# A decoder layer on one core, with 29 series of unread products behind its last output

## The chip, the cores and the metric

The kernel runs on one core of one Trainium2 chip. TensorE (PE) multiplies: its stationary operand is loaded by a weight load (PEld), its moving operand streams through, and the result goes to a bank of PSUM. VectorE (DVE), ScalarE (ACT) and GpSimd (POOL) work on elements; SyncE (SP) mostly issues DMAs. The metric is the device time of one execution in microseconds.

## The reference

The reference is one layer of a hybrid decoder on a sequence of 256 rows and a width of 2048: a combined projection, two groups of eight heads, an output projection, and a feed-forward part with a causal convolution of width 3.

```python
h = rmsnorm(x, pre_mix_gain)
q_sb, k_sb, v_sb, q_dl, k_dl, v_dl = split(h @ w_in)
o_sb = stick_breaking_attention(q_sb, k_sb, v_sb)
o_dl = dilated_attention(rope(q_dl), rope(k_dl), v_dl)
x = x + rmsnorm(concat(head_rmsnorm(o_sb), head_rmsnorm(o_dl)) @ w_out, post_mix_gain)
u = rmsnorm(x, pre_ffn_gain) @ w_up
gate, val = split(causal_conv3(u) + conv_b)
x = x + rmsnorm((gelu(gate) * val) @ w_down, post_ffn_gain)
```

## The kernel before

All matrices are float32. Each is split in two float32r parts, a high part wh (ACT copies the loaded tile, L89) and a low part wl (DVE subtracts, L96), and so are the activations; a product of the layer is then three products of TensorE: high by high, high by low, low by high. The weights stream in from memory in tiles of 128 x 1024 (SP's queue) and are consumed once, in this order: values, queries and keys with the attention between them, output projection, the up projection (chunks "up", mm_stationary at L98 to L112), and the down projection (class Down).

In mm_stationary the weights are the stationary operand: 128 columns of a high part against 512 moving columns (L111), and of a low part against 256 (L109). Low parts of the kinds "qk" and "up" start LOW_AT = 80 floats into their buffer; nothing else about L109's operands is shifted. In Down the weights move, 512 columns at a time, and the feed-forward activations are stationary: yp holds the two float32r parts of 13 pairs of blocks (yp0 the high ones, yp1 the low ones, 13 x 7 x 128 columns each), yt those of the single blocks. L629, L630 and L631 are the three products there. The bank of a product is of the pools ps_mm or ps_at, four banks each.

The end is written out by hand. The last units of the down projection are held back (HELD), and their products are made bank by bank, so that rows can be closed (L649), squared and scaled while the next bank is multiplied. The last bank is made in two halves of 256 columns, p9. The calls put() write the results and issue the stores (L693 and L695). Elsewhere a scheduler sets each engine's order from the program's text; instructions that go through pin() keep the order that they are written in.

Of the kernel before, what the change touches and what calls it, by code (L numbers as in the profile page):

```python
# [9 lines left out]
F32 = mybir.dt.float32  # L10
F32R = mybir.dt.float32r
BF16 = mybir.dt.bfloat16
# [4 lines left out]
P = 128  # L17
# [34 lines left out]
def layer_kernel(ctx: ExitStack, tc: tile.TileContext, a, out: bass.AP):  # L52
    nc = tc.nc
    V, A, T, G = nc.vector, nc.scalar, nc.tensor, nc.gpsimd
# [5 lines left out]
    ps_at = ctx.enter_context(tc.tile_pool(name="ps_at", bufs=4, space=PSUM))  # L60
# [206 lines left out]
    first = [None, None]  # L267
# [220 lines left out]
    phB = None  # L488
# [40 lines left out]
    class Down:  # L529
# [123 lines left out]
        def run(self):  # L653
# [89 lines left out]
            put(1, 1536, 2048, r, V, nc.scalar)  # L743
            pinned[0] = False

    down = Down()
    for i, (kind, p, s, _, w) in enumerate(chunks):
        parts = ahead(i, 0 if (kind, p, s) == ("out", 3, 3) else SPLITS)
        if kind == "v":
            if s == 0:  # L750
                pool, tag = (ps_at, "at") if p == 1 else (ps_mm, "mm")
# [26 lines left out]
        elif kind == "qk":  # L778
            ps = ps_mm.tile([P, 2, S], F32, tag="mm", name="mmqk")
# [9 lines left out]
        elif kind == "out":  # L789
# [14 lines left out]
            else:  # L804
                pinned[0] = True
                up0 = []
                r = [None, None]
# [94 lines left out]
                phB = ctx.enter_context(tc.tile_pool(name="phB", bufs=2))  # L902
                yt = [phB.tile([P, len(SINGLES), S], F32R, name=f"yt{i}", bufs=1) for i in range(2)]
                yp = [phB.tile([P, NPAIR, 7, P], F32R, name=f"yp{i}", bufs=1) for i in range(2)]
        else:
            ps = ps_mm.tile([P, 2, S], F32, tag="mm", name="mmu")
# [24 lines left out]
    rows = Rows(fg, "d", 5)  # L931
    tc.keep_in_program_order(A.preload_act_table_set("natural_log_exp_and_others"))
    down.run()


def _constants():
# [69 lines left out]
```

## Time and profile before

| what | us |
|---|---|
| median of 2 runs | 1094.28 |
| the runs | 1093.95 to 1094.6 |
| span of the profiled execution | 1092.2 |
| PE busy | 1079.7 |
| PE idle up to 400 us, and from there to 1083.33 | 3.7 and 0.1 |
| from PE's last start in the layer to the end of the span | 9.0 |

The profiled execution has a time of its own only as its span, from the first to the last instruction; the median of the runs lies 2.1 us above it. A row of the timeline has start, duration, engine, line, operation, the tiles written and read, and in brackets the idle time before it. A matmul's duration is its latency; several are in flight at once. A row that ends in x2 or more merges instructions that follow each other.

### The profile page before, as it was taken

The numbers are of one execution on the slowest core, as the hardware profiler recorded it, in microseconds if no ns is written. First come the engines' busy times: TensorE is split into PE (matmuls) and PEld (weight loads), VectorE is DVE, ScalarE is ACT, GpSimd is POOL, SyncE is SP. The second block draws the span as 40 slices with busy tenths as digits, with TensorE's granted clock in tenths as the row PEclk, the third lists the DMA queues.
The fourth block names the chain that finished last, engine by engine and source line by source line (L and its number), as shares of the span: only waits on it lengthen the run. The fifth ranks groups of instructions, "written<-read, shape, count | busy, mean of one in ns | idle before, by whom it ended". The sixth has DMA issues, their size and how long they took to land.

```text
span 1092.2 us, 16194 instructions
## 1 busy us (share of the span) xinstructions
PE 1079.7 (99%) x5855; PEld 932.8 (85%) x5855; DVE 878.4 (80%) x1371; ACT 668.4 (61%) x1046; POOL 5.3 (0%) x12
## 2 busy tenths in 40 slices
PE   9999999999999999999999999999999999999996
PEld 6898888988888888888888888888888888888885
DVE  6577776876876588988888888888888899889887
ACT  6656656656754476665666665666666566666665
POOL 0000000000000000000000000000000000000001
PEclk9999999999999999999999999999999999999998
DMA  8979768888889756656565656566556677767775
GB/s 309 391 255 310 275 231 305 266 283 288 265 274 307 260 191 212 193 194 193 193 193 193 193 193 193 193 193 194 193 193 193 216 235 249 253 219 249 250 242 209
DMA packets 75393, 257.79 MB, mean 236 GB/s; under 512 B 8496, under 2 KB 9520, under 8 KB 74544
## 3 DMA queue, kind: packets, MB, share of 16 engines
q1 hardware_dynamic: 74880, 256.22, 70.6%
q8 instruction: 46, 0.75, 0.3%
q10 hardware_dynamic: 432, 0.53, 0.1%
q14 instruction: 35, 0.29, 0.1%
HBM read 238.89 MB, written 17.83 MB: 235 GB/s over the span
## 4 chain that ended last, share of the span: by engine, by line
PE 97%; ACT 1%; issue 0%; DMA 0%; DVE 0%; SPq 0%; DVEq 0%; ACTq 0%
PE mmu L111 28%; PE mmu L109 14%; PE mmqk L111 11%; PE p L629 7%; PE p L630 7%; PE p L631 7%; PE mmqk L109 5%; PE mmo L151 3%; PE mmo L154 3%; PE mmo L150 3%; PE mmv L151 3%; PE mmv L154 3%; PE mmv L150 3%; PE mmu L117 1%; DMA raw<-in_w_v 0%
## 5 line engine op out<-in xcount | busy, mean ns | idle before, releaser
L96 DVE TENSOR_TENSOR wl<-raw,wh 128x1024 fp32r<-128x1024 f32 (+1 forms) x408 | 480.3, 1188 | 125.0 <-ACT wh L89 96.9
L89 ACT CAST wh<-raw 128x1024 fp32r<-128x1024 f32 (+1 forms) x408 | 414.2, 1024 | 171.5 <-PE mmu L111 42.3
L111 PE MATMUL mmu<-hT,wh 128*128 128x512 f32 x1344 | 318.2, 390 | 0.0
L111 PEld LDWEIGHTS mmu<-hT,wh 128*128 128x128 f32 x1344 | 249.2, 188 | 50.0
L109 PE MATMUL mmu<-hT,wl 128*128 128x256 f32 x1344 | 166.7, 276 | 0.0
L109 PEld LDWEIGHTS mmu<-hT,wl 128*128 128x128 f32 x1344 | 162.0, 188 | 3.5
L111 PE MATMUL mmqk<-hT,wh 128*128 128x512 f32 x512 | 121.8, 390 | 0.0
L111 PEld LDWEIGHTS mmqk<-hT,wh 128*128 128x128 f32 x512 | 94.9, 188 | 19.0
L502 ACT ACTIVATE cv<-u,par 128x256 f32<-128x256 f32 x86 | 51.9, 603 | 90.2 <-DVE u L500 90.0
L631 PE MATMUL p<-wl,yp 128*128 128x512 f32 x182 | 70.9, 390 | 0.0
L630 PE MATMUL p<-wh,yp 128*128 128x512 f32 x182 | 70.8, 389 | 0.0
L629 PE MATMUL p<-wh,yp 128*128 128x512 f32 x182 | 70.8, 389 | 0.0
L109 PE MATMUL mmqk<-hT,wl 128*128 128x256 f32 x512 | 68.3, 281 | 0.0
L109 PEld LDWEIGHTS mmqk<-hT,wl 128*128 128x128 f32 x512 | 63.8, 188 | 1.7
L503 DVE SCALAR_TENSOR_TENSOR cv<-u,par,cv 128x255 f32<-128x255 f32 x86 | 41.4, 481 | 29.0 <-ACT cv L502 29.0
L630 PE MATMUL p<-wh,yt 128*128 128x512 f32 (+1 forms) x140 | 53.6, 383 | 0.0
L629 PE MATMUL p<-wh,yt 128*128 128x512 f32 (+1 forms) x140 | 53.6, 383 | 0.0
L631 PE MATMUL p<-wl,yt 128*128 128x512 f32 (+1 forms) x140 | 53.5, 383 | 0.0
L135 ACT COPY half<-mmu 128x256 f32<-128x256 f32 x86 | 31.8, 370 | 35.2 <-PE mmu L109 21.7
L89 ACT CAST wh<-room 128x1024 fp32r<-128x1024 f32 x26 | 27.4, 1054 | 39.2 <-PE p L630 37.4
L150 PE MATMUL mmv<-wh,hT 128*128 128x512 f32 x128 | 49.8, 391 | 0.7 <-ACT hT L234 0.7
L151 PE MATMUL mmv<-wh,hT 128*128 128x512 f32 x128 | 50.0, 391 | 0.4 <-DVE hT L281 0.2
(178 smaller groups left out, 1248.2 us busy)
## 6 DMA issues: line engine op xcount, KB each, us to landing
raw<-in_w_up SPq DMA_DIRECT2D x172, 512.0 KB, 3.8
raw<-in_w_qk SPq DMA_DIRECT2D x64, 512.0 KB, 5.8
raw<-in_w_dn SPq DMA_DIRECT2D x60, 512.0 KB, 4.5
raw<-in_w_o SPq DMA_DIRECT2D x32, 512.0 KB, 4.8
raw<-in_w_v SPq DMA_DIRECT2D x28, 512.0 KB, 5.6
t<-in_w_dn SPq DMA_DIRECT2D x26, 512.0 KB, 5.0
t_kept<-t SPq DMA_DIRECT2D x26, 512.0 KB, 4.1
raw<-t_kept SPq DMA_DIRECT2D x26, 512.0 KB, 4.3
```

What stands on the lines that cost most here:

```text
L89: pin(A.copy(wh, raw))
L96: pin(V.tensor_tensor(wl, raw, wh.bitcast(F32), op=ALU.subtract))
L109: T.matmul(ps[:, 0, :], w, h[:, k, 0, :], **edge)
L111: T.matmul(ps, w, h[:, k, :, :], **edge)
L150: T.matmul(ps[t], hi[:, k, tc_], ws, start=(first and i == 0 and j == 0), stop=False)
L151: T.matmul(ps[t], lo[:, k, tc_], ws, start=False, stop=False)
L154: T.matmul(ps[t], hi[:, k, tc_], wl[:, j * 512:(j + 1) * 512], start=False, stop=(last and i == len(parts) - 1 and j == n - 1))
L502: A.activation(cv, u, AF.Identity, scale=cw(2), bias=par[:, P_CB + f:P_CB + f + 1])
L503: V.scalar_tensor_tensor(cv[:, 1:], u[:, :S - 1], cw(1), cv[:, 1:], op0=ALU.mult, op1=ALU.add)
L629: T.matmul(ps, yh, wh[:, cs], start=key not in self.begun, stop=False)
L630: T.matmul(ps, yl, wh[:, cs], start=False, stop=False)
L631: T.matmul(ps, yh, wl[:, cs], start=False, stop=self.left[key] == 0)
```

## The change

Behind down.run() the kernel calls a new function, more_products(). It takes one bank of ps_at (probe), clears a tile of bf16 zeros, and calls row() 29 times. A call makes 12 products (the first makes 24) that all write that bank; four moving places 2048 floats apart in yp0 take turns, and eight stationary places 1024 floats apart in yp1. The argument `at` moves the stationary operand by up to 112 floats. The moving operand is 512, 256 or 128 columns in one run; some series begin it 4, 8 or 16 floats further, some take it in two or four blocks with gaps, some read one block of 128 columns four times or one of 32 sixteen times, and one takes the zeros for both operands. All but the last two series set the start flag at their first product alone, and those two at each. The bank is read by nothing, and nothing of the layer is changed.

```diff
+    def more_products():
+
+        f0, f1 = (y.rearrange("p m r c -> p (m r c)") for y in yp)
+        ps = ps_at.tile([P, 512], F32, tag="at", name="probe")
+        zeros = phB.tile([P, 512], BF16, tag="cv0", name="zeros", bufs=1)
+        V.memset(zeros, 0.0)
+
+        def row(moving, at, n=12, first=False, w=None):
+            for i in range(n):
+                m = moving(2048 * (i % 4))
+                st = f1[:, at + 1024 * (i % 8):at + 1024 * (i % 8) + P] if w is None else w
...
+                T.matmul(dst, st, m, start=first or i == 0, stop=True, skip_group_check=True)
+
+        flat = lambda n, off=0: lambda b: f0[:, b + off:b + off + n]
+        blocks = lambda a, n, gap: lambda b: f0[:, b:b + a * gap].rearrange("p (a g) -> p a g", a=a)[:, :, 0:n]
+        same = lambda a, n: lambda b: f0[:, b:b + n].rearrange("p (o n) -> p o n", o=1).broadcast_to([P, a, n])
+        row(flat(512), 0, 24)
+        for at in (0, 16, 32, 48, 64, 80, 96, 112):
+            row(flat(512), at)
+        row(flat(512, 4), 0)
+        row(flat(512, 8), 0)
+        row(flat(512, 16), 16)
+        row(blocks(2, 256, 384), 0)
+        row(blocks(4, 128, 256), 0)
+        row(same(4, 128), 0)
+        row(same(16, 32), 0)
+        row(lambda b: zeros, 0, w=zeros[:, 0:P])
+        for at in (0, 16, 32, 48, 64, 80, 96, 112):
+            row(flat(256), at)
+        row(flat(128), 0)
+        row(flat(128), 80)
+        row(flat(512), 0, first=True)
+        row(flat(256), 80, first=True)
...
     down.run()
+    more_products()
```

In the built program, TensorE's queue before ends with the last products of the second half of bank p9 and the branch out of the program:

```order
L629 MATMUL p_10764<-wh,yt_4098 128x256
L630 MATMUL p_10764<-wh,yt_4099 128x256
L631 MATMUL p_10764<-wl,yt_4098 128x256
L629 MATMUL p_10764<-wh,yt_4098 128x256
L630 MATMUL p_10764<-wh,yt_4099 128x256
L631 MATMUL p_10764<-wl,yt_4098 128x256
L1002 UNCONDITIONAL_BRANCH
```

Behind the same last L631 there stand now the new products, of which the rows below are the first and the last (the zeros' products between them come one by one, each with a weight load of its own):

```order
L631 MATMUL p_10764<-wl,yt_4098 128x256
L763 MATMUL probe<-yp_4100,yp_4101 128x512 x204
L763 LDWEIGHTS zeros
L763 MATMUL probe<-zeros 128x512
...
L763 MATMUL probe<-yp_4100,yp_4101 128x256 x96
L763 MATMUL probe<-yp_4100,yp_4101 128x128 x24
L763 MATMUL probe<-yp_4100,yp_4101 128x512 x12
L763 MATMUL probe<-yp_4100,yp_4101 128x256 x12
L1043 UNCONDITIONAL_BRANCH
```

Nothing of the layer has moved at that end. The first of the new products waits for DVE, which has to read the first half of p9 (L649) out of the bank that probe gets; no later one waits for another engine but the first on the zeros, which needs their MEMSET.

That MEMSET the scheduler has put far ahead, on DVE, where the up projection gives way to the pairs of the down projection (room is the tile of sums, wl the low parts):

```order
 L612 TENSOR_TENSOR room_9001<-raw_9064,raw_8950 128x512
-L614 TENSOR_TENSOR room_9001<-room_9001,raw_9014 128x512
+L751 MEMSET zeros_10905 128x256
 L96 TENSOR_TENSOR wl_9072<-raw_8950,wh_9070 128x1024
 L96 TENSOR_TENSOR wl_9080<-raw_9014,wh_9078 128x512
+L614 TENSOR_TENSOR room_9001<-room_9001,raw_9014 128x512
 L96 TENSOR_TENSOR wl_9091<-raw_9064,wh_9089 128x1024
 L96 TENSOR_TENSOR wl_9101<-room_9001,wh_9099 128x1024
```

The MEMSET stands where L614 stood, and L614 has gone behind two L96. On TensorE, one L629 of bank p7 and one L631 of bank p5 have changed places a little later; DMAs and the other engines keep their order.

More of the change, by code (lines that the diff above doesn't have):

```diff
@@ L744, in run @@
             pinned[0] = False
+    def more_products():
[7 more added lines that the diff above has]
+                st = f1[:, at + 1024 * (i % 8):at + 1024 * (i % 8) + P] if w is None else w
+                cols = 1
+                for d in m.shape[1:]:
+                    cols *= d
+                dst = ps[:, 0:cols]
+                if len(m.shape) == 3:
+                    dst = dst.rearrange("p (a b) -> p a b", a=m.shape[1])
+                T.matmul(dst, st, m, start=first or i == 0, stop=True, skip_group_check=True)
[19 more added lines that the diff above has]
+        row(flat(256), 80, first=True)
     down = Down()
```

## The prediction

> **What bounds the kernel now.** I read four views in this order: the page's span and busy shares, to see which engine sets the length; the timeline of the last microseconds, since the change stands there; the timeline at four places where TensorE runs products of known widths, for the slot that one product takes; and the waits around 876 us, where the built program moves one DVE instruction. First the page:
>
> ```profile
> span 1092.2 us, 16194 instructions
> PE 1079.7 (99%) x5855; PEld 932.8 (85%) x5855; DVE 878.4 (80%) x1371; ACT 668.4 (61%) x1046; POOL 5.3 (0%) x12
> PEclk9999999999999999999999999999999999999998
> L111 PE MATMUL mmu<-hT,wh 128*128 128x512 f32 x1344 | 318.2, 390 | 0.0
> ```
>
> PE is busy 99% of the span at the full granted clock. The 390 ns of an L111 product is its latency, not its cost in a stream: the next one starts long before it ends. So a product is priced by the distance between starts. The end of the timeline, with the DVE read that frees the new products' bank:
>
> ```profile
> 1080.46 0.28 PE L629 MATMUL p<-wh,yt 128*128 128x256 f32 x1
> ...
> 1082.46 0.42 DVE L649 TENSOR_TENSOR room<-p,room 128x256 f32<-128x256 f32 x1
> ...
> 1083.21 0.28 PE L631 MATMUL p<-wl,yt 128*128 128x256 f32 x1
> ...
> 1085.76 2.06 DVE L693 SCALAR_TENSOR_TENSOR room<-room,rs,x1q 128x512 f32<-128x512 f32 x3
> ...
> 1087.20 1.00 ACTq L695 DMA_DIRECT2D out<-room  x2
> out<-room ACTq DMA_DIRECT2D x2, 256.0 KB, 2.5
> ```
>
> PE starts its last product at 1083.21. Behind it, 8.9 us pass without PE: DVE finishes the rows, the stores are issued until 1088.20 and land about 2.5 us later (last row, from the DMA view), near 1090.7; the span ends 1.5 us behind that. The new products stand on PE alone, and nothing of the layer waits for them.
>
> **What the change costs, part by part.** The program after it holds 360 more products: 216 of f32r 512 columns wide (the first series has 24, sixteen more have 12 each: 24 + 16 x 12), 108 of 256 columns (nine series), 24 of 128 (two), and 12 of bf16 512 columns on zeros (one); 29 calls of row in all. They are one queue on one engine, so the sum of their slots is the length of the block.
>
> Slots. These rows give them; starts are in the first column:
>
> ```profile
> 1060.04 0.39 PE L629 MATMUL p<-wh,yp 128*128 128x512 f32 x1
> ...
> 1074.32 0.39 PE L629 MATMUL p<-wh,yt 128*128 128x512 f32 x1
> 859.81 3.45 PE L109 MATMUL mmu<-hT,wl 128*128 128x256 f32 x29
> 67.25 0.59 PE L378 MATMUL z<-qk 128*128 128x256 f32 x2
> 67.68 0.38 PE L379 MATMUL z<-qk 128*128 128x128 f32 x2
> 67.90 0.22 PE L380 MATMUL z<-mskb,idb 128*128 128x128 bf16 x1
> 67.96 0.22 PE L381 MATMUL z<-mskb,idb 128*128 128x128 bf16 x1
> L109 PE MATMUL mmu<-hT,wl 128*128 128x256 f32 x1344 | 166.7, 276 | 0.0
> L378 PE MATMUL z<-qk 128*128 128x256 f32 x16 | 4.8, 380 | 0.0
> L379 PE MATMUL z<-qk 128*128 128x128 f32 x16 | 3.1, 274 | 0.0
> ```
>
> - 512 columns, f32r. From 1060.04 to 1074.32 stand 21 rounds of L629, L630, L631, 63 products: 14.28 / 63 = 0.2267 us. 216 x 0.2267 = 48.97 us.
> - 256 columns. Two prices. The 24 products from 1080.46 to 1083.21 make 23 slots: 2.75 / 23 = 0.1196 us. The 29 of L109 make 28 slots in 3.45 less the last one's 0.28: 0.1132 us. The difference between them that the code shows is the stationary operand's place: L109 loads low parts that LOW_AT puts 80 floats further. So the row at place 0 gets 0.1196 (12 products, 1.44 us), the two rows at place 80 get 0.1132 (24, 2.72 us), and the six other places the middle, 0.1164 (72, 8.38 us): 12.54 us. Bounds by the two prices: 12.2 and 12.9.
> - The same 6 ns could be saved by the 84 wide products at the seven places other than 0; no row has a wide product with its stationary there alone, so the bounds are 0 and 84 x 0.0064 = 0.54 us less, or as much more should a place be worse than 0. I take half of the saving, 0.27 less: 48.7 us for the wide ones.
> - 128 columns, f32r: the trace has none. Two bounds: the two L379 records start 0.38 - 0.27 = 0.11 us apart, the bf16 pair L380 and L381 0.06. I take 0.11, since f32 weights stand there as here: 24 x 0.11 = 2.64 us (1.44 by the lower; 2.87 if they cost as much as 256 columns, 0.1196).
> - bf16 zeros, 512 columns: between the f32r slot of 0.2267 and the 0.1196 of half the width. The two records of L378 start 0.59 - 0.38 = 0.21 apart; I take 0.22: 2.64 us (1.44 to 2.72).
> - Unseen patterns: moving operands begun 4, 8 and 16 floats further, in blocks with gaps (two rows), and one block read over and over (two rows). Every moving operand here is one plain run, so no row prices these. Below, they cost what a plain run does; above, I let an operand that is read badly take two slots: 12 x 0.2267 = 2.7 us a row, 19.0 us for all seven. I take nothing, because the slot of plain runs follows their width (0.2267 against 0.1196 for half), and these patterns have the same width.
>
> The block: 48.7 + 12.54 + 2.64 + 2.64 = 66.5 us.
>
> The Trainium skill, TensorE: Matmul & The Clock Gate, section Back-to-back issue gap, gives a warm slot of the columns over 2.4 per ns plus 2.5 ns: 216, 109 and 56 ns. By it, an estimate, the block would be 228 x 0.216 + 108 x 0.109 + 24 x 0.056 = 62.4 us, 4.1 less. Here the trace has 227 and 113 to 120 ns in f32r, so I go by the trace.
>
> Where the block starts. In the order, the first new product waits for one thing, the DVE read of bank p9 that begins at 1082.46 and takes 0.42 us; it is over at 1082.88, before the last product of the layer starts. So it starts one slot behind that one, at 1083.21 + 0.12 = 1083.33. All issue slots are over at 1083.33 + 66.5 = 1149.83. The last product's latency reaches 0.28 - 0.11 = 0.17 us further: 1150.0.
>
> What lies beside it. The stores, 8.9 us, now run under the block and cost nothing; their cover is 58 us deep. In exchange the program's end follows PE. What stands behind the last thing waited for is bounded by 0 and the 1.5 us that the span has behind the landing; these waits of SP lie in it:
>
> ```profile
> SPq L1002 <- DMA out<-room: 2.6, 1, 2.6
> SPq L1002 <- PEq L1002: 0.6, 2, 0.4
> ```
>
> The second row is SP meeting PE at the close, 0.6 us in two waits; I take 0.9 for the whole close. Span: 1150.9.
>
> The zeros. The MEMSET stands on DVE in the stretch where products of the pairs begin, and the scheduler has put L614 behind two L96 there, as the order shows. These rows are from before:
>
> ```profile
> L240 DVE MEMSET warm<- x1: 272/272/272, 0.9 to 0.9; 128x256 uint32 x1
> 875.55 0.69 DVE L614 TENSOR_TENSOR room<-room,raw 128x512 f32<-128x512 f32 x1
> 876.16 2.96 DVE L96 TENSOR_TENSOR wl<-raw,wh 128x1024 fp32r<-128x1024 f32 x3
> 877.26 1.05 ACT L89 CAST wh<-room 128x1024 fp32r<-128x1024 f32 x1
> 877.43 0.19 PEld L631 LDWEIGHTS p<-wl,yp 128*128 128x128 f32 x1 [0.29 <-DVE wl L96]
> ```
>
> PEld waits 0.29 us for an L96 there. In place of a 0.69 us L614, a 0.27 us MEMSET now stands ahead of it, so it can come 0.42 us sooner and the wait can go. L614 comes about 1.5 us later (0.27 and two L96), and the CAST of room that waits for it with it; its products are two units further on, which covers that. Bounds: -0.3 (the wait goes) and +0.3 (the CAST is late next). I take 0. The swap of an L629 and an L631 of two banks on PE moves no work; also 0.
>
> Sum: the span grows by 1150.9 - 1092.2 = 58.7 us. The profiled execution is 1092.2 and the median of the runs 1094.28, 2.1 above; I keep that distance. Forecast: 1094.3 + 58.7 = **1153.0 us**, 5.4% slower.
>
> **The rivals.**
>
> 1. Patterns or places read badly. If one to three of the rows with unseen patterns take double slots, 2.7 to 8.2 us are added: 1155.7 to 1161.2. If all seven do, 1172. For it: no row shows such a pattern, and 6 ns hang on a place already. Against it: the price needed is forty times that.
> 2. The small prices all fall at their lower ends: 84 x 0.0064 off the wide rows at new places (half of it is in already), 256 columns at 0.1132, 128 at 0.06, zeros at 0.12: -0.27 - 0.3 - 1.2 - 1.2, about 1150.0. By the gap rule above, 1148.9; there the place of an operand would have to explain the whole 10 ns between 216 and 227 in every row, but rows at place 0 are what the 227 was measured on.
> 3. The other side, not slower: the products do not run. The block would have to shrink to 1092.2 + 21.9 - 0.9 - 0.17 - 1083.33 = 29.7 us to stay within 2%, 0.083 us a product on average; the narrowest kind alone takes 0.11. Only dropping them gets there, since their bank is never read: 1094.3. Against it: the built program holds all 360 behind the last L631. Nor can earlier waits swallow them: up to 1083.33 PE idles only about 3.6 us.
> 4. The clock falls to half for the block: another 66 us, 1219. The PEclk row shows a fall only in the last slice, where PE has nothing; here PE does not stop.
>
> **How the numbers follow.** The forecast with its small bounds (1150.0 to 1155): 0.77. Rival 1: 0.15 for one to three rows, 0.03 for more. Rival 2 below 1150.0, the gap rule in it: 0.03. Rival 3: 0.01. Rival 4: 0.01. The range takes in the small ends and rival 1 up to three rows: 1149 to 1161, which leaves out about 0.1. A measurement of this kernel tells 2%, some 22 us, from no change. Slower: 0.985; within: 0.01; faster: 0.005, for something unforeseen.
>
> **What would show it.** After: PE's products rise by 360 records, 6215 in all; L631's last start stays near 1083.2 and the first new one follows within 0.2 us; the wide rows go at 0.220 to 0.230 us, 256 columns at 0.113 to 0.120, 128 at 0.11; PE's last end lies near 1150, the last store lands where it did, and the span ends some 0.9 us behind PE. The wait of L631 at 877.43 shrinks or stays. Wrong would be: a row whose slots are far off 0.227 (rival 1; the row says which operand), slots of 0.06 at 128 columns, a granted clock under 1.00 in the block, a start held back by a wait.

## The result and the profile after

The changed kernel takes 1153.85 us, the median of two runs from 1153.58 to 1154.12, against 1094.28: a ratio of 1.0548, with a 95% interval of 1.0531 to 1.0565. The forecast was 1153.0.

The page of the changed kernel, its first lines:

```profile
span 1152.3 us, 16914 instructions
PE 1148.0 (100%) x6215; PEld 990.0 (86%) x6215; DVE 878.7 (76%) x1372; ACT 668.0 (58%) x1046; POOL 6.7 (1%) x12
DVE  6577766868866789888888888888889888988600
ACT  6656646646644576655656656656556666666400
L763 PE MATMUL probe<-yp,yp 128*128 128x512 f32 (+2 forms) x348 | 65.6, 350 | 0.0
```

PE has 360 products more, and DVE one instruction. The two digit rows show where the time went: DVE and ACT are done in the last two slices, some 58 us, in which only PE works. The next rows are of PE's timeline, around the start of the block and at its end:

```profile
1083.38 0.28 PE L630 MATMUL p<-wh,yt 128*128 128x256 f32 x1
1083.50 0.28 PE L631 MATMUL p<-wl,yt 128*128 128x256 f32 x1
1083.62 0.86 PE L763 MATMUL probe<-yp,yp 128*128 128x512 f32 x3
...
1150.27 1.22 PE L763 MATMUL probe<-yp,yp 128*128 128x256 f32 x9
```

The block begins one narrow slot behind the last product of the layer, at 1083.62; the row has no idle time in brackets, so no wait stands ahead of it. The nine products of the last row begin at 1150.27 and are over 1.22 us later, at 1151.49. Who waits for that, the waits of SP's queue tell (what waited and for what; us in total, times, the longest):

```profile
SPq L1043 <- PE probe L763: 60.2, 1, 60.2
SPq L695 <- DVE room L649: 10.0, 1, 10.0
SPq L1043 <- DMA out<-room: 2.6, 1, 2.6
...
SPq L1043 <- PEq L1043: 0.6, 2, 0.4
```

The wait for the stores is 2.6 us as before. Behind it SP now waits 60.2 us for the last new product, and then the same 0.6 us of closing waits follow. The stores have moved nowhere; they are simply no longer last.

Each window below holds one series of the block, from its first start to that of the next (so 12 slots; the x counts products in flight at the edges too). The columns are the window, its length, PE's busy time with the number of products, the granted clock, and the DMAs:

```profile
1089.08:1091.80 2.72, 2.72 (x13) 1.00 0.52 191
1091.80:1094.59 2.79, 2.79 (x13) 1.00 0.01 3
1097.39:1100.14 2.75, 2.75 (x13) 1.00 0.00 0
1111.21:1114.00 2.79, 2.79 (x13) 1.00 0.00 0
1119.52:1122.25 2.73, 2.73 (x13) 1.00 0.00 0
1127.69:1130.53 2.84, 2.84 (x13) 1.00 0.00 0
1130.53:1132.95 2.42, 2.42 (x13) 1.00 0.00 0
```

They are, in this order, the wide products at place 0, at 16 and at 48, the moving operand 4 floats further, two blocks with a gap, 32 columns read sixteen times, and the zeros. Over twelve slots, 2.72 us is 0.2267, 2.79 is 0.2325 and 2.84 is 0.2367. No pattern takes a second slot, and the clock is 1.00 throughout. All series follow, with the mean distance of starts within each, in ns. In four of them, the zeros, 256 columns at place 0, 128 columns at place 0 and the last one of 512 columns, the first distance belongs to the change from one kind of product to the next (227, 308, 59 and 289 ns) and is left out of the mean:

```
512 columns, place 0 (24, then 12)      227.9   226.6
512 columns, places 16 32 48 64         233.5   233.0   228.9   227.7
512 columns, places 80 96 112           233.5   233.0   228.9
moving +4, +8; both +16                 232.5   233.4   226.9
2 blocks of 256, 4 of 128 with gaps     227.7   226.6
128 four times, 32 sixteen times        226.6   236.5
zeros, bf16                             216
256 columns, places 0 16 32 48          119     117.8   119.1   117.7
256 columns, places 64 80 96 112        119.3   117.8   119.1   117.7
128 columns, places 0 and 80            111.7   111.6
start at each: 512 at 0, 256 at 80      227     117.8
```

The wide slots repeat after 64 floats: 16 and 80 agree, 32 and 96, 48 and 112. Where both operands are shifted by 16 floats, the slot here is that of place 0.

### The profile page after: what moved, and what is told of

Read it like the earlier page. It is cut to its first block, busy times and chain, and to the rows that moved or that the text cites. A ratio compares the mean times of both kernels' runs of the same rounds, so it can differ in the third digit from the quotient of the medians.

```text
span 1152.3 us, 16914 instructions
## 1 busy us (share of the span) xinstructions
PE 1148.0 (100%) x6215; PEld 990.0 (86%) x6215; DVE 878.7 (76%) x1372; ACT 668.0 (58%) x1046; POOL 6.7 (1%) x12
## 4 chain that ended last, share of the span: by engine, by line
PE 97%; DMA 1%; ACT 1%; issue 0%; DVE 0%; SPq 0%; ACTq 0%
PE mmu L111 26%; PE mmu L109 13%; PE mmqk L111 10%; PE p L631 6%; PE p L630 6%; PE p L629 6%; PE probe L763 6%; PE mmqk L109 5%; PE mmo L151 3%; PE mmo L154 3%; PE mmo L150 3%; PE mmv L154 2%; PE mmv L150 2%; PE mmv L151 2%; DMA mg<-in_xT 1%; PE mmu L117 1%
## 5 line engine op out<-in xcount | busy, mean ns | idle before, releaser
L96 DVE TENSOR_TENSOR wl<-raw,wh 128x1024 fp32r<-128x1024 f32 (+1 forms) x408 | 480.2, 1187 | 125.3 <-ACT wh L89 96.9
L89 ACT CAST wh<-raw 128x1024 fp32r<-128x1024 f32 (+1 forms) x408 | 414.0, 1024 | 170.1 <-PE mmu L111 42.7
L109 PE MATMUL mmu<-hT,wl 128*128 128x256 f32 x1344 | 166.7, 277 | 0.0
L109 PEld LDWEIGHTS mmu<-hT,wl 128*128 128x128 f32 x1344 | 162.1, 188 | 3.5
L631 PE MATMUL p<-wl,yp 128*128 128x512 f32 x182 | 70.9, 390 | 0.0
L629 PE MATMUL p<-wh,yp 128*128 128x512 f32 x182 | 70.8, 389 | 0.0
L109 PE MATMUL mmqk<-hT,wl 128*128 128x256 f32 x512 | 68.3, 281 | 0.0
L763 PE MATMUL probe<-yp,yp 128*128 128x512 f32 (+2 forms) x348 | 65.6, 350 | 0.0
L109 PEld LDWEIGHTS mmqk<-hT,wl 128*128 128x128 f32 x512 | 63.8, 188 | 1.7
L763 PEld LDWEIGHTS probe<-yp,yp 128*128 128x128 f32 x348 | 56.1, 188 | 9.1
L629 PE MATMUL p<-wh,yt 128*128 128x512 f32 (+1 forms) x140 | 53.6, 383 | 0.0
L631 PE MATMUL p<-wl,yt 128*128 128x512 f32 (+1 forms) x140 | 53.5, 383 | 0.0
```

The lines of the kernel that those rows point to most:

```text
L89: pin(A.copy(wh, raw))
L96: pin(V.tensor_tensor(wl, raw, wh.bitcast(F32), op=ALU.subtract))
L109: T.matmul(ps[:, 0, :], w, h[:, k, 0, :], **edge)
L629: T.matmul(ps, yh, wh[:, cs], start=key not in self.begun, stop=False)
L631: T.matmul(ps, yh, wl[:, cs], start=False, stop=self.left[key] == 0)
L763: T.matmul(dst, st, m, start=first or i == 0, stop=True, skip_group_check=True)
```

## Experiments

All kernels below keep the layer as it is and differ only behind it. They replace the body of more_products by calls of one helper, in which ss and ms are the steps of the stationary and of the moving places, in floats:

```diff
+        def series(n, cols, at, ss=1024, ns=8, ms=2048, nm=4, off=0, stop=True):
+            for i in range(n):
+                m = f0[:, off + ms * (i % nm):off + ms * (i % nm) + cols]
+                st = f1[:, at + ss * (i % ns):at + ss * (i % ns) + P]
+                T.matmul(ps[:, 0:cols], st, m, start=i == 0, stop=stop or i == n - 1, skip_group_check=True)
```

The theory at the start was that of the prediction: the time is the sum of the slots, less what the stores cover. Its first rival was that nothing is covered, or that the products slow the closing rows. Open were the layer's end, which came 0.29 us later than in the trace of before, and the place: at 80 the narrow products took 0.1178 us and not the 0.1132 of L109.

**The kernel before, once more.** No edit.

> The kernel before, once more, for the spread of its own trace. If the layer's end moves from execution to execution, its last product starts anywhere between 1083.1 and 1083.6 us here; if the 0.29 us by which the layer ended later in the changed kernel is the change's doing (the clearing of the zeros on DVE), it starts at 1083.2 again, within 0.05.

Its span is 1092.3 us, and its last product starts here:

```profile
1083.35 0.28 PE L631 MATMUL p<-wl,yt 128*128 128x256 f32 x1
```

The same program started that product at 1083.21 in one trace and at 1083.35 in the other, so 0.14 us move by themselves. The two kernels that follow, also without the clearing of the zeros, start it at 1083.05 and 1082.93. Traces without the clearing thus differ by 0.42 us, more than the 0.29 in question. Where the 0.29 arose, the traces tell too. The first and the third row are of the changed kernel, the second is of the kernel before (where the first product stands at 67.25, as the prediction shows):

```profile
67.48 0.59 PE L378 MATMUL z<-qk 128*128 128x256 f32 x2
872.19 0.39 PE L629 MATMUL p<-wh,yp 128*128 128x512 f32 x1
872.48 0.39 PE L629 MATMUL p<-wh,yp 128*128 128x512 f32 x1
```

PE is 0.23 us behind at the first of these products and 0.29 at the second, both ahead of the MEMSET at 875.81. The delay is not the MEMSET's doing; what makes it vary is not known.

**Short blocks: 24 and 48 products.** The zeros and all other series are gone.

```diff
-        row(flat(512), 0, 24)
...
+        series(24, 512, 0)
```

> Only the first series of 24 wide products is left, without zeros. Theory (a sum of slots on one engine, beside the stores): 24 x 0.2267 = 5.4 us behind 1083.3 end near 1089.1, before the stores land at some 1091.3, so the time is that of before within 0.5 us. Rival (products slow the closing rows or the stores, or the end always waits for them in full): 5.4 us more, 1099.7.

> 48 wide products in one series, without zeros. Theory: 48 x 0.2267 = 10.9 us end at 1094.4, the close takes 0.8 to 0.9, so the span is 1095.3, 3.1 more than before, and the time about 1097.3. Rival (no cover): 10.9 us more, 1105.2.

With 24 products the median is 1094.04 us over ten runs against 1093.93 over sixteen of the kernel before on that chip, a ratio of 1.0002 (0.9993 to 1.0011): no difference. With 48 it is 1097.06 over seven, a ratio of 1.0029 (1.0018 to 1.0041): 3.1 us. The waits of SP's queue, with 24 first and then with 48:

```profile
SPq L695 <- DVE room L649: 10.0, 1, 10.0
SPq L1016 <- DMA out<-room: 2.6, 1, 2.6
SPq L695 <- DVE room L693: 2.3, 4, 0.8
```

```profile
SPq L1016 <- PE probe L755: 3.4, 1, 3.4
SPq L1016 <- DMA out<-room: 2.6, 1, 2.6
```

With 24 there is no wait for probe at all; with 48 one of 3.4 us stands behind the stores. 24 products cost 5.4 us of PE and nothing in time that these runs can tell, the next 24 cost 3.0 us, and that is the cover of the closing rows and stores running out. The rival without cover, 1099.7 and 1105.2, falls.

**Places, steps and flags.** This kernel and those that follow it were timed once each; their slots are read from one trace. The list, for 512 and for 256 columns:

```diff
+            for ss, ns in ((1024, 8), (128, 12), (0, 1)):
+                for ms, nm in ((2048, 4), (512, 12), (0, 1)):
+                    for at in (0, 16, 32, 48, 80):
+                        series(12, cols, at, ss, ns, ms, nm)
+            for at in (0, 16, 80):
+                series(12, cols, at, 128, 12, 512, 12, stop=False)
+            for at in range(0, 64, 4):
+                series(12, cols, at, 128, 12, 512, 12)
+            for at in range(0, 64, 16):
+                series(12, cols, at, 128, 12, 512, 12, off=at)
```

> 136 series of 12 products instead of 29: stationary places 1024, 128 or 0 floats apart, moving places 2048, 512 or 0 floats apart, at five shifts of the stationary operand; then steps and shift as in L109 with stop set at the last product alone; then shifts of 4 floats from 0 to 60; then both operands shifted alike; all at 512 and at 256 columns. In all 816 wide products by 0.2267 to 0.2335 us and 816 narrow ones by 0.113 to 0.120 us: 277 to 288 us, a span of 1361 to 1373. For the narrow slot at 80, 0.1132 in L109 and 0.1178 in the changed kernel: by the theory of steps it is 0.113 with steps of 128 and 512 and 0.118 with 1024 and 2048; by the theory of flags it is 0.113 only where stop is left off; by the theory of buffers (other memory) none gives 0.113. For the wide slot: if only the distance of both operands modulo 64 floats counts, it is 0.2266 at 0, 0.2335 at 16 and 80, 0.233 at 32 and 0.229 at 48 for all steps, and 0.2266 where both are shifted alike; if the steps count, these differ among the nine pairs of steps.

The span is 1369.0 us, and the block takes 284.7 from its first to its last start; both are in the forecast. The slots in ns (mean without the first distance of a series), with three of the nine pairs of steps, whose others agree within 0.8, but for 1.2 at wide place 0 in the very first series:

```
512 columns            0      16     32     48     80
steps 1024 and 512     227.7  233.3  233.3  228.5  233.3
steps 128 and 512      227.7  233.3  233.3  228.5  233.3
steps 0 and 0          227.7  233.3  233.3  228.6  233.4
stop at the last       227.6  233.3                233.3
256 columns            0      16     32     48     80
steps 1024 and 512     120.0  117.7  119.0  117.7  113.4
steps 128 and 512      120.0  117.7  119.0  117.7  113.4
steps 0 and 0          120.0  117.7  119.0  117.8  113.3
stop at the last       120.0  117.8                117.7
256, shifts of 4 from 0 to 60:  120.0 118.2 118.2 117.7 113.7 118.8 119.0 119.8
                                118.2 119.8 120.2 118.1 117.7 116.8 116.7 120.0
```

Four windows of 12 narrow slots show it, with steps of 128 and 512 in each: place 80, place 80 with stop at the last, place 16 in the list of steps, and place 16 among the small shifts. Behind them stand two wide series with both operands shifted alike, by 0 and by 16 floats:

```profile
1305.70:1307.06 1.36, 1.36 (x15) 1.00 0.00 0
1338.12:1339.54 1.42, 1.42 (x15) 1.00 0.00 0
1301.44:1302.86 1.42, 1.42 (x15) 1.00 0.00 0
1345.23:1346.60 1.37, 1.37 (x14) 1.00 0.00 0
1260.80:1263.52 2.72, 2.72 (x14) 1.00 0.00 0
1263.52:1266.28 2.76, 2.76 (x13) 1.00 0.00 0
```

One part of the expectation failed. Where both operands are shifted alike, the wide slot was to be 226.6, and it is 226.6 at a shift of 0 but 230.7, 230.8 and 230.7 at 16, 32 and 48. That is less than the 233 of the stationary operand shifted alone by 16 or 32, so the moving operand's place counts too; that the distance of the two alone counts is not shown.

Steps do not matter, and flags do not either in the wide series. But the narrow ones refute all three theories on them: at 80 the slot is 113.4 with every step, and 117.7 where stop is left off; at 16 it is 117.7 in the list of steps, and 113.7 in that of small shifts, with the same steps and flags as one of the former. What differs is the series ahead: 80 follows 48 in the list of steps, but 16 with stop left off and 64 in the changed kernel; 16 follows 12 among the small shifts, and 0 elsewhere. So the new theory was that of history.

**What leads a series.**

```diff
+        for rep in range(2):
+            for cols in (256, 512):
+                for at in (0, 16, 32, 48):
+                    for pc in (256, 512):
+                        for pa in range(0, 64, 4):
+                            series(4, pc, pa)
+                            series(10, cols, at)
+        for pa in (0, 64):
+            series(6, 256, pa)
+            series(48, 256, 80)
+        series(6, 512, 0)
+        series(48, 256, 80)
+        series(6, 256, 12)
+        series(48, 256, 80)
+        data = phB.tile([P, 512], BF16, tag="cv0", name="data", bufs=1)
+        V.tensor_copy(data, f0[:, 0:512].bitcast(F32))
+        for i in range(12):
+            T.matmul(ps, data[:, 0:P], data, start=i == 0, stop=True, skip_group_check=True)
```

> No series of the change; instead 256 pairs of series, each 4 products at a leading place (0 to 60 floats in steps of 4, 256 or 512 columns) and 10 at a place of 0, 16, 32 or 48 (256 or 512 columns), the whole list twice; then four series of 48 narrow products at 80 behind leaders at 0 and 64 (narrow), 0 (wide) and 12 (narrow); then 12 bf16 products of 512 columns on data that are not zeros. Some 650 us in all. Theory of history: the narrow slot at 16 and at 80 takes one of two values, 0.1133 and 0.1178, set by the leading series; a pair gives the same value in both lists, and a series of 48 keeps the value that it begins with. Rival, the place alone: all series at 16 give one value. Rival, drift: the value changes between the two lists or within a series of 48. Wide products: by history some leaders give less than 0.2266 at one of the places; by place alone 0.2266, 0.2333, 0.2330 and 0.2286 whatever leads. The bf16 products: 0.216 if the type sets that slot, 0.227 if the zeros did.

The block takes 1280 us; my 650 counted the list once where it runs twice. The two lists agree within 0.8 ns in every pair. In ns (mean without the first two distances, in which a series may still settle), narrow products at place 16, by the place of the leader, in the first list and in the second:

```
leader narrow, 0 to 28   117.7/117.7 113.3/113.4 113.3/113.3 113.4/113.4 113.3/113.3 113.4/113.4 113.4/113.4 113.4/113.4
leader wide, 0 to 28     117.6/117.9 113.4/113.4 117.7/117.7 117.9/117.7 113.4/113.3 113.4/113.6 115.4/115.4 117.9/117.9
```

One place takes two steady values, and with the same products ahead the same value comes again. (The 115.4 is a mean over a series that settles late.) How far back the past counts is not shown, since both lists have the same order beyond the four leaders too. That four are not all of it, the run before suggests: a narrow leader at 16 gives 113.3 here, while there the series at 80 with stop at the last, which stands behind one at 16, took 117.7. That series has no counterpart with stop at each product and the same series ahead, so for narrow products the flag is not ruled out as a part of it. The windows below, with columns as above, are two of the series of 48 at place 80, behind a wide leader at 0 and behind a narrow one at 12, 47 slots each, and then the bf16 products:

```profile
2348.04:2353.58 5.54, 5.54 (x49) 1.00 0.00 0
2354.41:2359.74 5.33, 5.33 (x49) 1.00 0.00 0
2359.86:2362.25 2.39, 2.39 (x14) 1.00 0.00 0
```

5.54 / 47 is 0.1179 and 5.33 / 47 is 0.1134 (the starts themselves give 0.1178 and 0.1134), and each is held to the end of its series: no drift. History stands for the narrow products, the place alone falls. For the wide ones neither form of the expectation holds. They never went below 226.6 whatever led; at place 0 they took 226.6 to 231.6, at 48 228.4 to 233.4, and at 16 always 232.7 to 233.9. So the place sets most of the wide slot, and what led adds up to 5 ns at 0 and at 48. The bf16 products take 216 on data as on the zeros, so the type sets that slot and not the zeros.

In the layer itself, L109's series of low parts are at 0.1134 nearly always, but two of the 73 with 15 products or more stay at 0.1176 and 0.1179 (the first distance of each left out). The 0.1132 that the prediction took for a price of place 80 was one of two states of it.

**Widths.** The term for 128 columns had no row of its own; it went by weight loads.

```diff
+        widths = (32, 64, 128, 192, 224, 256, 320, 384, 448, 512)
+        for at in (0, 16):
+            for cols in widths:
+                series(12, cols, at)
...
+        for cols in widths:
+            for i in range(12):
+                T.matmul(ps[:, 0:cols], data[:, 0:P], data[:, 0:cols], start=i == 0, stop=True, skip_group_check=True)
```

> Instead of the change's series, ten widths from 32 to 512 columns, 12 products each: f32r at place 0, f32r at place 16, then bf16 on data that are not zeros. Theory (a product's slot is the longer of its weight load and its columns): f32r takes 0.110 to 0.113 us at 32, 64, 128 and 192 columns alike, 0.113 to 0.120 at 224 and 256, and from 320 on its columns over 2400 per us plus 0.010 to 0.020 (0.147, 0.175, 0.200 and 0.227 at place 0); bf16, with its shorter load, follows its columns down to 128 (0.056 there, 0.109 at 256, 0.216 at 512). Rival (columns set the slot at every width): f32r at 64 takes about 0.04, at 128 about 0.06, at 192 about 0.09. All together 46 to 49 us by the theory, 40 to 43 by the rival.

The block takes 53.8 us, more than both theories give. f32r takes 0.1117 us at 32 columns and at 64 alike, and 0.147, 0.174 and 0.202 to 0.207 at 320, 384 and 448; bf16 takes 0.056 at 128 columns, 0.109 at 256 and 0.216 at 512, and 0.025 at 32. The rival falls, and the theory of loads fits, with one thing left open: every product here has a load of its own, so no run tells the load from another fixed cost of an f32r product. But f32r at 192 and 224 columns takes 0.2133, against at most 0.113 and 0.120 expected. These are the windows of 32, 64, 128, 192, 224 and 320 columns at place 0, in this order:

```profile
1083.62:1084.88 1.26, 1.26 (x14) 1.00 0.96 387
1084.88:1086.22 1.34, 1.34 (x14) 1.00 0.80 274
1086.22:1088.01 1.79, 1.79 (x15) 0.75 0.53 184
1088.01:1090.62 2.61, 2.61 (x13) 0.50 0.93 350
1090.62:1093.21 2.59, 2.59 (x14) 0.50 0.01 3
1094.97:1096.74 1.77, 1.77 (x15) 1.00 0.00 0
```

The column before the last two is the granted clock: it falls to 0.50 while PE's records show no gap, and at half the clock the slot is 0.2133 where it was 0.1117, 1.9 times as long. The same happened a second time, behind the narrow products at place 16. This is the fall of the clock in rival 4 of the prediction, which I had given 1 in 100 because "PE does not stop".

**When the clock falls.**

```diff
+        for cols in (224, 192, 128, 96, 64, 32):
+            series(90, cols, 0)
+            series(66, 512, 0)
```

> Instead of the change's series, six series of 90 narrow products at place 0, of 224, 192, 128, 96, 64 and 32 columns, each followed by 66 wide ones (15 us). In the run of the widths the granted clock stood at 0.50 for 6.83 us twice, each time beginning some 3 us into the products of 32 and 64 columns, with PE never idle. Theory (the clock follows the columns that stream): at 0.112 us a product the columns fill 83, 71, 48, 36, 24 and 12% of the slots; the clock falls in the series of 64 and 32, stays at 1.00 in those of 224 and 192, and 128 and 96 tell where between. Rival (the clock follows the weight loads, which fill every slot alike): it falls in all of them or in none. A series without a fall takes 90 x 0.112 to 0.118 = 10.1 to 10.6 us, one with a fall of 6.83 us about 3.4 us more, and the wide series behind it may lose some of that instead. All together 150 us without a fall, up to 170 with six.

The block takes 172.7 us. The windows are the narrow series of 224, 192, 128 and 96 columns, the wide one behind that, and those of 64 and 32:

```profile
1083.01:1093.06 10.05, 10.05 (x93) 1.00 0.57 210
1108.06:1118.09 10.03, 10.03 (x91) 1.00 0.01 2
1133.13:1143.13 10.00, 10.00 (x91) 1.00 0.01 2
1158.19:1173.99 15.80, 15.80 (x92) 0.61 0.00 1
1173.99:1191.31 17.32, 17.32 (x67) 0.86 0.00 1
1191.31:1206.17 14.86, 14.86 (x91) 0.65 0.00 0
1222.85:1238.46 15.61, 15.61 (x92) 0.62 0.00 1
```

The three wider series run 90 products at 0.1117 us and a clock of 1.00, the three narrower ones fall. The bf16 slots grow by 106.8 ns from 256 to 512 columns, 0.417 ns a column; by that, columns fill 48% of the slots at 128 and 36% at 96, so in this run the limit lies between. All of them load weights alike, so the rival falls. Results written to the bank grow with the columns as well, and no run tells the two apart. The clock's records, with start, length and granted share:

```
1161.78  17.07  0.50
1195.91  13.65  0.50
1226.63  17.07  0.50
```

The falls lasted 13.65 and 17.07 us, not 6.83, and ran on into the wide products behind, which took 0.426 us each until the clock came back. So the sum missed its upper end of 170, and the length of a fall is not one value.

## Why the prediction was right, point by point

**PE alone sets the block, and nothing stands ahead of it.** Right: the first new product follows the last L631 by one slot, 0.12 us, and SP waits 60.2 us for the last.

**The start, 1083.33.** It was 1083.62. Without the change the layer's last product started at 1083.21 and 1083.35 in two traces, and in the short blocks at 1082.93 and 1083.05; and PE was already 0.29 us behind at 872.48, ahead of the MEMSET. So this is spread and not the change.

**The zeros' MEMSET, taken as 0 within 0.3.** Right in size, and by both mechanisms that were named, one of which I had thought covered. These rows of the changed kernel are the new order on DVE and what it did to the loads of PE:

```profile
875.81 0.27 DVE L751 MEMSET zeros<- 128x256 uint32 x1
877.50 0.19 PEld L631 LDWEIGHTS p<-wl,yp 128*128 128x128 f32 x1
877.96 0.68 DVE L614 TENSOR_TENSOR room<-room,raw 128x512 f32<-128x512 f32 x1
878.75 1.05 ACT L89 CAST wh<-room 128x1024 fp32r<-128x1024 f32 x1 [1.10 <-DVE room L614]
881.12 0.19 PEld L631 LDWEIGHTS p<-wl,yp 128*128 128x128 f32 x1 [0.21 <-DVE wl L96]
```

The load that waited 0.29 us at 877.43 now waits for nothing at 877.50. L614 comes at 877.96 in place of 875.55, the CAST of room waits 1.10 us for it, and further on a load waits 0.21 us for the L96 behind that CAST. Against the trace of before, PE gains 0.10 us at the first place and loses 0.09 behind it, most of it at the second.

**The wide products, 48.7 us.** 49.65, which is 0.95 too little in the forecast. The nearest row alone, 216 x 0.2267, gives 48.97. The step that failed is "The same 6 ns could be saved by the 84 wide products": the saving of L109 does not carry over. Places 16, 32, 80 and 96 cost 6 to 7 ns more than place 0, and 48 and 112 cost 2. The prediction had "as much more should a place be worse than 0" among its bounds, and took the saving. Seven of the 17 wide rows lie above the 0.220 to 0.230 us that it gave as a sign.

**The narrow products, 12.54 us.** 12.78. The two prices, read rightly from their rows, were taken for two places; the runs show that place 80 has both 0.1133 and 0.1178, by what led, and in this block it took the higher.

**128 columns, 2.64, and zeros, 2.64.** 2.68 and 2.60. The reasons were tested as well: f32r at 32 and 64 columns takes the same 0.1117, so not the columns set it but a fixed cost, by the argument above the load; and bf16 takes 0.216 on zeros and on data.

**Unseen patterns, taken as plain runs.** Right within 10 ns a product. The dearest, 32 columns read sixteen times, takes 0.2365, not two slots; a moving operand 4 or 8 floats further takes 0.2325 and 0.2334. These three rows add 0.27 us, which is part of the 0.95 above. Rival 1 did not happen, and with 6215 records none of the products was dropped, as rival 3 had it.

**Cover and close.** The stores covered 7.8 us of the 10.9 that 48 products take (10.9 less the 3.1 measured); the forecast's sum had 1092.2 - 0.9 - 0.17 - 1083.33 = 7.8. The close took 0.8 us (1151.49 to 1152.3) against 0.9.

**The sum.** The span was forecast at 1150.9 and came out at 1152.3: 0.3 from the start, 1.2 from the block, 0.1 less from the close. The profiled execution took 1154.12, 1.8 above its span, where I had kept 2.1, the distance of a median from the span of one run. So the 0.85 us between 1153.0 and the median flatter the sum: the span was 1.4 short, and 0.3 of that was made up by this distance and 0.3 by the other run, which was faster than the profiled one. That is luck.

**The rule on the slot.** The Trainium skill, TensorE: Matmul & The Clock Gate, section Back-to-back issue gap, gives the columns over 2.4 per ns plus 2.5, for an isolated product as it says. The bf16 series, each product with a load of its own, agree with it to the ns: 56, 109 and 216. The f32r series do not; they carry 10 to 21 ns more at 512 columns and stay at 0.1117 from 32 to 224 columns, where the clock holds. So by that rule the block, 62.4 us where 67.7 were measured, would have come out 5.3 us short.

**The clock.** It stayed at 1.00, as forecast, but my reason was too weak. Series of 90 products of 64 columns dropped it with no gap on PE, so an unbroken queue is not enough.

## What to carry to other kernels

Price work that is added to one engine's queue by the distance between starts of its nearest kin, not by durations, and take off what fits beside work that already stood at the end: here 24 products were free and the next 24 were not. A slot that differs by a few ns in two rows need not differ by what the code shows there; before it is used as a price of that, look whether one and the same row has both values. Short f32r products here took 0.1117 us whatever their width, each with a weight load of its own, and runs of them at 96 columns or less also halved the clock; at 128 columns and more it held.

## What the runs showed of the hardware

- The slot of a f32r product follows the place of its stationary operand and repeats after 64 floats: at 512 columns 226.6 ns and more at 0, 232.7 to 233.9 at 16, 228.4 to 229.4 behind most leads at 48. The place of the moving operand counts too (both shifted by 16: 226.9 in one run and 230.7 in another). Steps do not count, and flags do not at 512 columns.
- At one place there are several steady slots, and the products ahead choose: at 16 and at 80 narrow ones take 113.4 or 117.8 ns, at 80 for 48 products on end. Why, and how many products back, no run here shows.
- The granted clock falls to 0.50 with no gap in PE's records, in series whose columns fill 36% of the slots or less, and not at 48%. The falls began 3.5 to 4.6 us into such products, and lasted 6.83, 13.65 and 17.07 us. The Trainium skill, TensorE: Matmul & The Clock Gate, Part 1, says that the gate goes by how busy PE was in a free-running window of 3.4 us; the lengths are 2, 4 and 5 of these, which agrees, and busy has to be read here as something that grows with the columns, not as a queue without gaps.
